# Transposing 20 of 48 groups of softmax numerators on VectorE and GpSimd instead of TensorE, in a four-layer decoder trunk

## The chip, the cores and the metric

The kernel runs on one core of a Trainium2 chip. The metric is the device time of one execution in microseconds. Runs of one kernel agree within about 0.2%. Profiles come from one further execution with the hardware profiler on.

## What is computed

A residual stream of 256 rows by 1024 columns in float32 goes through four layers, each a token mixer and a squared-ReLU MLP. Mixers 0 and 3 are differential attention (8 heads, each the difference of two softmaxes), mixer 1 is block-sparse attention whose block is as long as the sequence, so that only causal attention is left of it (16 heads), and mixer 2 is attention in a window of 128 with sinks (16 heads on 2 key heads).

```python
def reference(x, positions, ...):
    cos, sin = rope_tables(positions)
    h = x
    for i in range(DEPTH):
        a = rms_norm(h, attn_norm_g[i])
        y = (diff_attention, moba_attention, swa_sink_attention)[i % 3](a, ..., cos, sin)
        h = h + y
        h = h + sqrelu_mlp(rms_norm(h, mlp_norm_g[i]), mlp_w_up[i], mlp_w_down[i])
    return rms_norm(h, final_norm_g)

# differential attention, per head and block of queries
    p = jax.nn.softmax(jnp.where(causal, s, -jnp.inf), axis=-1)
    p = p[:, :, 0] - lam * p[:, :, 1]
    o = jnp.einsum('bhqk,bkhe->bqhe', p.astype(v.dtype), v)
    o = rms_norm(o, sub_g) * (1.0 - lambda_init)
```

(The mixers are picked by a tuple here for brevity, and "..." stands for the parameters.)

## The kernel before, in words

All large products are float32 as two parts of a shorter type: for each piece of weights (`raw`, 128 x 1024, brought by one DMA of SyncE's queue) ScalarE writes the high part `whi`, and VectorE subtracts it to get the low part `wlo`. TensorE multiplies three combinations of parts. The two splits, 374 of each, are the steady work of ScalarE and VectorE through the whole kernel. TensorE multiplies from a layer's input projection (`p_in`), through attention, output projection (`p_d`), and MLP (`p_up`, `p_down`), to the next.

Attention lies inside the input projection of its layer: its small steps are put between the projection's matmuls. One step of attention handles one head of a `Diff` layer, or one block of two heads of a `Heads` layer (eight blocks). It goes so:

- `rope` (L589, VectorE: `ropea`, two of `ropeb`, and an addition) turns the first 16 columns of each head's queries and keys, for four heads or blocks at once; `turn` (L694, TensorE) brings queries and keys to columns, in bank `p_qk`; `Queries` (L707) and `put_keys` (L735) split them in high and low parts (`qh`, `qhl`, `kpad`, `kboth`). VectorE makes the low parts; `copied` (L689) puts copies of the high parts beside them, on ScalarE or GpSimd.
- `scores` (L608): TensorE multiplies (`p_s`), VectorE adds the mask and takes the row's least (`ns`, `nm`), ScalarE takes the exponential (`e`) and the sums.
- A `Diff` head combines its two softmaxes on VectorE into one set of numerators, a `Heads` block divides each of its two by its sum (`rl`, on ScalarE or VectorE). One set of numerators is three squares of 128 x 128, since the causal upper square is left out: the tile `e` holds 128 x 384 of them. This is the "group" of the title. There are 8 in layer 0, 16 in layer 1, 16 in layer 2 and 8 in layer 3, 48 in all.
- `turned` (L658): the values are multiplied along the keys, so the group must be transposed. TensorE makes three 128 x 128 transposes into the bank `p_t`, and ScalarE or VectorE copies them out of PSUM to the tile `et`.
- `pair` (L794 for `Diff`, L899 for `Heads`): TensorE multiplies `et` with the values of two heads or blocks into `p_av`. A `Heads` pair is split and stored in `oo` for the output projection; a `Diff` pair is normed by a power that GpSimd takes (`ry`), scaled (`o`), transposed (`p_o`) and stored.

The order is made by a planner, `Plan` (L66). Each piece of work is a task with an engine, a cost, predecessors and a lag after its end; rooms in memory (`et`, `e`, `wk` for PSUM banks, and others) are tokens that a task takes and a later one gives back. `either` and `copied` name tasks with two possible engines. `forth` (L85) builds the order forward in time, choosing for each engine the ready task with the earliest due time, `back` (L148) works out the due times from the end, and the table `EARLIER` shifts the due time of single tasks, by their number. `run` (L177) then issues every task in the order of its planned start. `Ordered` (L198) keeps that order in the program, which is why nearly every instruction bears the line L208. The hardware runs each engine's queue in that order and waits on semaphores alone. The constants `MOVE`, `LATE` and `ASIDE` stand in the file of before without use.

Of the kernel before, what the change touches and what calls it, by code (L numbers as in the profile page):

```python
# [18 lines left out]
P = 128  # L19
# [17 lines left out]
MARGIN = 56  # L37
OWN = 0.08
MOVE = (1.82, 1.95)
LATE = 4.0  # L40
ASIDE = ((0, 2), (0, 1, 2, 3, 4, 5), ())
EARLIER = {4: -7.2, 63: -6, 67: -6.2, 130: -1.4, 132: 3.1, 702: 0.7, 2508: 7.4, 2574: -1.3, 2675: -2.1, 4095: -0.9,
           4105: -5.225, 4107: -23.3, 4167: -3.1, 4176: 4, 4179: -7.9, 4180: 10.7, 4196: -23.9, 4270: 0.9, 4296: -7.5,
           4306: -5.2, 4309: -1.1, 4443: -7.1, 7311: 2.4}


def f(ap):
# [167 lines left out]
def trunk(ctx: ExitStack, tc: tile.TileContext, xT, gains, lams, swa_row, fng, weights, out):  # L215
# [19 lines left out]
    def r3(n):  # L235
        return lambda t: t.rearrange("p (a b) -> p a b", a=n)

    plan = Plan({"wk": range(4), "acc": range(2), "raw": range(RAW), "w": range(SPLIT), "e": (4, 5),
                 "et": (6, 7, 12, 13), "q": (2, 3), "o": range(2), "ns": range(2), "sq": range(2)})
    add, give = plan.add, plan.give  # L240


# [20 lines left out]
    def pe(cost, do, after=(), rank=1, **kw):  # L263
        return add("PE", cost, do, after, rank=rank, **kw)
# [393 lines left out]
    def turned(e, to, after):  # L658

        st = {}  # L660

        def do():
            st["p"] = bank("p_t")
            for j in range(3):
                transpose(st["p"][:, P * j:P * j + P], e()[:, 1 + P * j:1 + P * j + P])

        a = pe(0.36, do, after, take={"wk": 1})
        b = either((0.39, 0.48), lambda: A.activation(to(), st["p"][:, :3 * P], AF.Copy),
                   lambda: V.tensor_copy(to(), st["p"][:, :3 * P]), [a])
        give("wk", [b], a)  # L670
        return a, b

    class Keys:

# [82 lines left out]
    class Diff:  # L757
# [4 lines left out]
        def head(self, h, q, k, after):  # L762
            g, l1 = h // 2, {}

            def begin():
                if g not in self.l0:
                    self.l0[g] = tiny.tile([P, 2, NT], F32, tag="l0", name="l0", bufs=3)
                l1[0] = tiny.tile([P, NT], F32, tag="l", name="l", bufs=6)

            st, exps, first = scores(q, k, True, causal, None, lambda c: l1[0] if c else self.l0[g][:, h % 2], after, begin)  # L770

            def combine():
                c2 = tiny.tile([P, NT], F32, tag="c2", name="c2")
# [17 lines left out]
            self.ready[h], self.turn[h] = b, a  # L791
            return first

        def pair(self, g, v, after):  # L794
            st = {}

            def values():
                p = st["p"] = bank("p_av")
                for h in range(2):
                    et = self.et[2 * g + h]  # L800
                    o = [p[:, S * h + P * t:S * h + P * t + P] for t in range(NT)]
                    matmul(o[0], et[:, 0:P], v(2 * g + h, 0), True, True)
                    matmul(o[1], et[:, P:2 * P], v(2 * g + h, 0), True, False)
                    matmul(o[1], et[:, 2 * P:3 * P], v(2 * g + h, 1), False, True)

            def squares():
                ss = st["ss"] = tiny.tile([P, 2 * NT], F32, tag="ss", name="ss")
                for t in range(2 * NT):
                    junk = sb.tile([P, P], F32, tag="junk", name="junk", bufs=1)
                    A.activation(junk, st["p"][:, P * t:P * t + P], AF.Square, accum_out=ss[:, t:t + 1])  # L810

            def means():
                l0 = self.l0[g][:, :, :].rearrange("p a b -> p (a b)")
                el = tiny.tile([P, 2 * NT], F32, tag="el", name="el")
                V.scalar_tensor_tensor(el, l0, EPS, l0, op0=OP.mult, op1=OP.mult)
                V.scalar_tensor_tensor(st["ss"], st["ss"], 1.0 / P, el, op0=OP.mult, op1=OP.add)

            def power():
                st["y"] = tiny.tile([P, 2 * NT], F32, tag="ry", name="ry")
                G.tensor_tensor(st["y"], st["ss"], minus_half, op=OP.pow)  # L820

            def scaled():
# [35 lines left out]
    class Heads:  # L858
# [4 lines left out]
        def head(self, b, q, k, after):  # L863
            st2 = {}

            def begin():
                st2["l"] = tiny.tile([P, 2, NT], F32, tag="l", name="l", bufs=6)

            st, exps, first = scores(q, k, True, self.mask, self.sinks and self.sinks(b), lambda c: st2["l"][:, c], after, begin)
            ends, a = [], None  # L870
            for c in range(2):

                def inverse(c=c):
                    if c == 0:
                        st2["rl"] = tiny.tile([P, 2, NT], F32, tag="rl2", name="rl2", bufs=4)
# [7 lines left out]
                def to(c=c):  # L883
                    if (b // 2, c) not in self.et:
                        self.et[b // 2, c] = room(self.turn[b // 2, c].got["et"][0], [P, 2, 3 * P], "et")
                    return self.et[b // 2, c][:, b % 2]
# [4 lines left out]
                if b % 2 == 0:  # L891
                    z.take["et"] = 1
                    self.turn[b // 2, c] = z
                ends.append(z)
                self.ready[b, c] = y
            give("e", ends, first)
            return first

        def pair(self, g, v, shared, after):  # L899
            st = {}  # L900

            def values():
                p = st["p"] = bank("p_av")
                o = r3(2)(p)
                for m, cols in ((0, slice(0, S)), (1, slice(P, S))):
                    k = slice(S * m, S * m + S - P * m)
                    for b in (None,) if shared else range(2):
                        for c in range(2):
                            r, et = slice(HD * c, HD * c + HD), self.et[g, c]
# [12 lines left out]
            a = pe(1.5, values, [*(self.ready[2 * g + b, c] for b in range(2) for c in range(2)), *after],  # L922
                   take={"wk": 1})
            for c in range(2):
                give("et", [a], self.turn[g, c])
# [481 lines left out]
```

## Time and profile before

| quantity | value |
|---|---|
| median of 3 runs (lowest, highest) | 1127.94 us (1127.61, 1129.84) |
| the profiled execution, its own time | 1128.46 us |
| its span in the trace | 1126.7 us |
| granted TensorE clock, mean | 0.999 |
| VectorE busy | 826.7 us, 73% |
| ScalarE busy | 671.0 us, 60% |
| GpSimd busy | 54.1 us, 5% |
| splits: `wlo` on VectorE, `whi` on ScalarE | 443.0 us, 373.9 us |

The profile names engines PE (TensorE), DVE (VectorE), ACT (ScalarE), POOL (GpSimd) and SP (SyncE). A row of a timeline gives the start, the length, the engine and line, the operation with the tile it writes, an arrow and what it reads, the shape, and how many instructions stand in the row ("x4"). A bracket behind it gives the idle time of that engine ahead of the row and what ended it. Rows of groups give the count, then the busy time and the mean of one in ns, then the idle time ahead. Matmuls are pipelined and the lengths of their rows are modelled, so distances between starts say more than lengths.

### The profile page before, as it was taken

Reading aid. Unit: us, or ns where it says so; the run is one execution under the profiler, and the core shown is the slowest. Engines: PE = TensorE matmul, PEld = TensorE weight load, DVE = VectorE, ACT = ScalarE, POOL = GpSimd, SP = SyncE. Lnnn points to the kernel's source line nnn. Section 1 sums busy time; section 2 is a strip of 40 time slices with the busy share of each in tenths; the row PEclk is TensorE's granted clock in tenths of the full one; section 3 lists DMA queues with packets and bytes.
Section 4 is the critical chain, followed back from the end, with each engine's and each line's share of the span. In section 5 each row is a group of like instructions: output and inputs, shape, how many; then the busy total and the mean of one; then the engine's idle time right before and its main releaser. Section 6 shows DMA issues by size and latency. Waiting matters only on the chain.

```text
span 1126.7 us, 16639 instructions
## 1 busy us (share of the span) xinstructions
PE 1117.2 (99%) x6462; PEld 978.6 (87%) x6462; DVE 826.7 (73%) x1396; ACT 671.0 (60%) x1163; POOL 54.1 (5%) x89
## 2 busy tenths in 40 slices
PE   9999999999999999999999999999999999999997
PEld 7889888888888898888888898888888899888886
DVE  8986987656697688765569898765669777877453
ACT  6996665444497765554457965553548776555342
POOL 1010000000100000000011100000010110100000
PEclk9999999999999999999999999999999999999999
DMA  8445455555444455455544265555543544556541
GB/s 313 181 153 172 174 201 185 200 192 187 150 154 150 155 181 209 169 215 175 202 173 145 77 229 189 186 193 204 179 171 123 177 161 177 187 187 206 193 144 38
DMA packets 30031, 198.65 MB, mean 176 GB/s; under 512 B 3456, under 2 KB 4864, under 8 KB 6528
## 3 DMA queue, kind: packets, MB, share of 16 engines
q1 hardware_dynamic: 29664, 197.19, 50.0%
q8 instruction: 51, 0.84, 0.3%
q10 hardware_dynamic: 288, 0.39, 0.1%
q14 instruction: 28, 0.23, 0.1%
HBM read 196.52 MB, written 1.05 MB: 175 GB/s over the span
## 4 chain that ended last, share of the span: by engine, by line
PE 98%; DMA 0%; ACT 0%; issue 0%; DVE 0%; POOLq 0%; POOL 0%; SPq 0%; DVEq 0%
PE p_up L208 32%; PE p_down L208 24%; PE p_in L208 20%; PE p_d L208 8%; PE p_last L208 7%; PE p_s L208 2%; PE p_av L208 2%; PE p_t L208 1%; PE p_qk L208 1%; DMA raw<-in_weights 0%; PE p_o L208 0%; PE p_res L208 0%; ACT hg L208 0%; ACT sq L208 0%; POOLq L1403 0%
## 5 line engine op out<-in xcount | busy, mean ns | idle before, releaser
L208 DVE TENSOR_TENSOR wlo<-raw,whi 128x1024 fp32r<-128x1024 f32 (+1 forms) x374 | 443.0, 1218 | 200.8 <-ACT whi L208 195.8
L208 ACT ACTIVATE whi<-raw 128x1024 fp32r<-128x1024 f32 (+1 forms) x374 | 373.9, 1043 | 249.4 <-issue 90.7
L208 PE MATMUL p_up<-hg,whi 128*128 128x512 f32 x1024 | 240.2, 391 | 0.0
L208 PEld LDWEIGHTS p_up<-hg,whi 128*128 128x128 f32 x1024 | 189.5, 188 | 37.9 <-DVE hg L208 0.7
L208 PE MATMUL p_in<-whi,hg 128*128 128x512 f32 (+1 forms) x672 | 188.6, 393 | 1.1 <-DVE hg L208 1.1
L208 PE MATMUL p_down<-uu,whi 128*128 128x512 f32 x768 | 179.1, 390 | 0.0
L208 PEld LDWEIGHTS p_down<-uu,whi 128*128 128x128 f32 x768 | 142.7, 188 | 28.5
L208 PEld LDWEIGHTS p_in<-whi,hg 128*128 128x128 f32 x672 | 122.1, 189 | 23.9 <-DVE hg L208 1.8
L208 PEld LDWEIGHTS p_up<-hg,wlo 128*128 128x128 f32 x1024 | 127.6, 192 | 2.8
L208 PE MATMUL p_up<-hg,wlo 128*128 128x256 f32 x1024 | 128.5, 283 | 0.0
L208 PE MATMUL p_in<-wlo,hg 128*128 128x512 f32 (+1 forms) x336 | 105.4, 392 | 0.0
L208 ACT ACTIVATE uu<-u 128x512 fp32r<-128x512 f32 x64 | 40.2, 628 | 99.2 <-DVE u L208 99.2
L208 PEld LDWEIGHTS p_down<-uu,wlo 128*128 128x128 f32 x768 | 95.3, 192 | 1.9
L208 PE MATMUL p_down<-uu,wlo 128*128 128x256 f32 x768 | 95.9, 283 | 0.0
L208 PE MATMUL p_d<-oo,whi 128*128 128x256 f32 x512 | 95.2, 287 | 0.0
L208 PEld LDWEIGHTS p_d<-oo,whi 128*128 128x128 f32 x512 | 79.6, 192 | 1.1 <-issue 0.9
L208 PE MATMUL p_last<-whi,uu 128*128 128x512 f32 x256 | 79.1, 390 | 0.0
L208 PE MATMUL p_d<-oo,wlo 128*128 128x256 f32 x256 | 72.5, 283 | 0.0
L208 PEld LDWEIGHTS p_in<-wlo,hg 128*128 128x128 f32 x336 | 61.6, 188 | 11.6 <-DVE wlo L208 0.2
L208 ACT ACTIVATE e<-ns,nm 128x128 f32<-128x128 f32 (+3 forms) x128 | 56.9, 447 | 4.5 <-DVE nm L208 3.3
L208 DVE TENSOR_TENSOR uu<-u,uu 128x512 fp32r<-128x512 f32 x64 | 44.1, 689 | 20.4 <-ACT uu L208 19.7
L208 PEld LDWEIGHTS p_last<-whi,uu 128*128 128x128 f32 x256 | 48.1, 188 | 10.0
(158 smaller groups left out, 1030.1 us busy)
## 6 DMA issues: line engine op xcount, KB each, us to landing
raw<-in_weights SPq DMA_DIRECT2D x183, 1024.0 KB, 4.8
raw<-in_weights SPq DMA_DIRECT2D x8, 256.0 KB, 4.9
hT<-in_xT SPq DMA_DIRECT2D x8, 128.0 KB, 4.5
out<-last SPq DMA_DIRECT2D x2, 320.0 KB, 2.4
bias<-in_swa_row SPq DMA_DIRECT2D x1, 512.0 KB, 5.7
grow<-in_fng SPq DMA_DIRECT2D x1, 512.0 KB, 4.9
out<-last ACTq DMA_DIRECT2D x2, 192.0 KB, 2.3
lv<-in_lams SPq DMA_DIRECT2D x1, 256.0 KB, 10.5
```

What stands on the lines that cost most here:

```text
L208: x = getattr(self.engine, name)(*args, **kw)
```

## The change

The constant `ASIDE`, which now is used, names heads 0 to 3 of layers 0 and 3 (`Diff`) and blocks 0 to 5 of layer 1; layer 2 has none. For a head or block in the list, the new class `Aside` takes the place of `turned`: VectorE transposes the group within 32 x 32 squares, straight from `e` into a tile `squares` of which there is one, and GpSimd then moves each square to its place in `et`, four copies for each of four bands of 32 rows, so 16 for a head (32 x 96 elements each) and 16 for a block, after both of its transposes (32 x 192 each). So 4 + 12 + 4 = 20 groups leave TensorE. In the planner the value products are held back by `LATE`, 2.5 us behind the last copy.

The columns of `et` are in an order that suits these copies, and all groups of a layer are read in that order: the value products take strided operands. In layer 2 a pair's value products, formerly one matmul for both blocks, become one for each block. Some small tiles get more buffers, `EARLIER` is another table (two of its numbers are shown), and the space set aside for dynamic DMA is halved. No DMA is added or taken away.

```diff
-LATE = 4.0
-ASIDE = ((0, 2), (0, 1, 2, 3, 4, 5), ())
-EARLIER = {4: -7.2, 63: -6, ...}
+LATE = 2.5
+ASIDE = ((0, 1, 2, 3), (0, 1, 2, 3, 4, 5), ())
+EARLIER = {23: -3.7, 727: -0.5, ...}
...
+    class Aside:
+        def __init__(self, heads, to):
+            self.heads, self.to, self.s, self.squares = heads, to, None, []
+        def turn(self, c, e, after):
+            def do():
+                if self.s is None:
+                    self.s = sb.tile([P, 4, self.heads * 3, 32], F32, tag="turn", name="squares", bufs=1)
+                V.transpose(self.s[:, :, 3 * c:3 * c + 3].rearrange("p k j q -> p j k q"),
+                            e()[:, 1:1 + 3 * P].rearrange("p (j k q) -> p j k q", j=3, k=4))
+            t = dve(384, do, after, 0.08, take=None if self.squares else {"turn": 1})
+            self.squares.append(t)
+            return t
+        def move(self):
+            last = []
+            for a in range(4):
+                def do(a=a):
+                    to = self.to()
+                    for k in range(4):
+                        G.tensor_copy(to[32 * k:32 * k + 32, a], self.s[32 * a:32 * a + 32, k])
+                last.append(add("POOL", MOVE[self.heads - 1], do, [*self.squares, *last[-1:]],
+                                take=None if last else {"et": 1}))
+            give("turn", last, self.squares[0])
+            return last[0], add("POOL", 0.0, lambda: None, last, lag=LATE)
...
-            a, b = turned(lambda: st["e"][:, 0], to, [a])
-            a.take["et"] = 1
+            if h in ASIDE[0]:
+                x = Aside(1, lambda: to().rearrange("p (j a q) -> p a j q", j=3, a=4))
+                a = x.turn(0, lambda: st["e"][:, 0], [a])
+                self.turn[h], self.ready[h] = x.move()
+            else:
...
-                z, y = turned(lambda c=c: st["e"][:, c], to, [z, self.turn.get((b // 2, c))])
+                if aside:
+                    z = aside.turn(c, lambda c=c: st["e"][:, c], [z])
+                else:
+                    z, y = turned(lambda c=c: st["e"][:, c], lambda c=c: to_part(c), [z, self.turn.get(b)])
...
+            if aside:
+                self.turn[b], self.ready[b, 0] = aside.move()
+                self.ready[b, 1] = None
...
-                            if shared:
-                                matmul(o[r, :, cols], v(m, c), et[:, :, k], m == 0, m == 1)
+                            et = self.et[2 * g + b].rearrange("p (a c j q) -> p a c j q", a=4, c=2, j=3)
+                            x = v(m, c if shared else 2 * (2 * g + b) + c)
+                            if m:
+                                matmul(o[r, b, :, 1], x, et[:, :, c, 2], False, True)
                             else:
-                                matmul(o[r, b, cols], v(m, 2 * (2 * g + b) + c), et[:, b, k], m + b == 0, m == 1)
+                                matmul(o[r, b], x, et[:, :, c, 0:2], b == 0, False)
```

Counts of instructions, before and now: on TensorE 144 and 84 transposes into `p_t`, and 16 and 32 value products in layer 2. On VectorE 17 and 7 copies of `et`, no and 20 transposes into `squares`, 14 and 6 scalings of numerators. On ScalarE 31 and 21 copies of `et`, 50 and 58 scalings, 6 and 14 copies of `qhl`, 24 and 20 of `kboth`. On GpSimd 26 and 18 copies of `qhl`, none and 4 of `kboth`, none and 224 of `et`.

The rows below show the order on VectorE in layer 1, shortly ahead of the work for block 4's queries; numbers behind names count the tiles, `raw57` is a piece of weights, `oo` belongs to the pair of blocks ahead, and "waits" lists the counters that an instruction waits for. Before:

```order
L208 TENSOR_TENSOR oo_3470<-p_av_3448,oo_3470 128x2x256 [waits Activation_49]
L208 TENSOR_TENSOR oo_3474<-p_av_3461,oo_3474 128x2x256 [waits Activation_49]
L208 TENSOR_TENSOR wlo57_3495<-raw57_3260,whi57_3494 128x1024 [waits DMAHW1_49,PE_49,Activation_49]
L208 TENSOR_TENSOR wlo57_3495<-raw57_3260,whi57_3494 128x1024 [waits Activation_49]
L208 TENSOR_TENSOR ropea_3539<-qk_3527,cc_126 128x256 [waits Activation_49]
L208 TENSOR_TENSOR ropeb_3540<-qk_3527,nsn_128 128x16x8
L208 TENSOR_TENSOR ropeb_3540<-qk_3527,sn_127 128x16x8
L208 TENSOR_TENSOR qk_3527<-ropea_3539,ropeb_3540 128x16x16 [waits DVE_49]
```

And now:

```order
L207 TENSOR_TENSOR wlo57_3518<-raw57_3302,whi57_3517 128x1024 [waits Activation_49]
L207 STREAM_TRANSPOSE squares_3556<-e_3441 128x3x4x32 [waits DVE_49,Activation_49,Pool_49]
L207 TENSOR_TENSOR oo_3558<-p_av_3538,oo_3558 128x2x256 [waits Activation_49]
L207 TENSOR_TENSOR ropea_3597<-qk_3585,cc_126 128x256 [waits Activation_49]
L207 TENSOR_TENSOR ropeb_3598<-qk_3585,nsn_128 128x16x8
L207 TENSOR_TENSOR ropeb_3598<-qk_3585,sn_127 128x16x8
L207 TENSOR_TENSOR qk_3585<-ropea_3597,ropeb_3598 128x16x16 [waits DVE_49]
L207 STREAM_TRANSPOSE squares_3556<-e_3441 128x3x4x32
```

A block's first transpose, which waits for GpSimd (`Pool`), has moved in ahead of `rope`; the second stands behind it.

The second place is VectorE further on in layer 1, ahead of the scores of block 6, whose queries and keys are `qhl` and `kboth`. Before:

```order
L208 COPY et_3704<-p_t_3673 128x384
L208 TENSOR_TENSOR ropea_3714<-qk_3696,cc_126 128x256 [waits Activation_49]
L208 TENSOR_TENSOR ropeb_3715<-qk_3696,nsn_128 128x16x8
L208 TENSOR_TENSOR ropeb_3715<-qk_3696,sn_127 128x16x8
L208 TENSOR_TENSOR qk_3696<-ropea_3714,ropeb_3715 128x16x16 [waits DVE_49]
L208 TENSOR_TENSOR wlo60_3712<-raw60_3478,whi60_3711 128x1024 [waits DMAHW4_49,PE_49,Activation_49]
L208 SCALAR_TENSOR_TENSOR qhl_3740<-p_qk_3729,qh_3739 64x2x256 [waits Activation_49]
L208 SCALAR_TENSOR_TENSOR qhl_3740<-p_qk_3729,qh_3739 64x2x256
L208 TENSOR_TENSOR kboth_2984<-p_qk_3734,kpad_2983 64x2x256 [waits PE_49,Activation_49]
L208 TENSOR_TENSOR kboth_2984<-p_qk_3734,kpad_2983 64x2x256
```

And now:

```order
L207 RECIPROCAL rl2_3762<-l_3707 128x2 [waits Activation_49]
L207 TENSOR_TENSOR wlo59_3654<-raw59_3463,whi59_3653 128x1024
L207 STREAM_TRANSPOSE squares_3816<-e_3706 128x3x4x32 [waits Activation_49,Pool_49]
L207 SCALAR_TENSOR_TENSOR qhl_3813<-p_qk_3794,qh_3812 64x2x256 [waits Activation_49]
L207 SCALAR_TENSOR_TENSOR qhl_3813<-p_qk_3794,qh_3812 64x2x256
L207 TENSOR_TENSOR kboth_3036<-p_qk_3801,kpad_3035 64x2x256 [waits PE_49,Activation_49]
L207 TENSOR_TENSOR kboth_3036<-p_qk_3801,kpad_3035 64x2x256
L207 STREAM_TRANSPOSE squares_3816<-e_3706 128x3x4x32
```

Here too a transpose that waits for GpSimd stands directly ahead of the queries and keys, where a subtraction of weights stood.

The third place is GpSimd in layer 3, from its first copies of queries to the last power; an ISA row without a tile changes GpSimd's code library. Before:

```order
L208 CAST qhl<-qh 64x2x256 x4
L208 ISA
L208 TENSOR_TENSOR ry<-ss,minus_half 128x4 x2
L208 CAST qhl<-qh 64x2x256 x4
L208 TENSOR_TENSOR ry<-ss,minus_half 128x4 x2
```

And now:

```order
L207 CAST qhl<-qh 64x2x256 x2
L207 COPY et<-squares 32x3x32 x12
L207 CAST kboth<-kpad 64x2x256 x2
L207 COPY et<-squares 32x3x32 x36
L207 ISA
L207 TENSOR_TENSOR ry<-ss,minus_half 128x4
L207 COPY et<-squares 32x3x32 x16
L207 TENSOR_TENSOR ry<-ss,minus_half 128x4
L207 CAST qhl<-qh 64x2x256 x2
L207 TENSOR_TENSOR ry<-ss,minus_half 128x4 x2
```

The change of library stood behind two pairs of casts; it now stands behind the copies of three heads, and the fourth head's copies stand between the first two powers.

More of the change, by code (lines that the diff above doesn't have):

```diff
@@ L238, in trunk @@
     plan = Plan({"wk": range(4), "acc": range(2), "raw": range(RAW), "w": range(SPLIT), "e": (4, 5),
-                 "et": (6, 7, 12, 13), "q": (2, 3), "o": range(2), "ns": range(2), "sq": range(2)})
+                 "et": (6, 7, 12, 13), "q": (2, 3), "o": range(2), "ns": range(2), "sq": range(2), "turn": range(1)})
     add, give = plan.add, plan.give
@@ L665, in do, with put @@
                 transpose(st["p"][:, P * j:P * j + P], e()[:, 1 + P * j:1 + P * j + P])
+        def put(copy):
+            o, x = to(), st["p"][:, :3 * P]
+            copy(o, x.rearrange("p (j m) -> p j m", j=3) if len(o.shape) == 3 else x.rearrange("p (j a q) -> p j a q", j=3, a=4))
         a = pe(0.36, do, after, take={"wk": 1})
-        b = either((0.39, 0.48), lambda: A.activation(to(), st["p"][:, :3 * P], AF.Copy),
-                   lambda: V.tensor_copy(to(), st["p"][:, :3 * P]), [a])
+        b = either((0.39, 0.48), lambda: put(lambda o, x: A.activation(o, x, AF.Copy)), lambda: put(V.tensor_copy), [a])
         give("wk", [b], a)
         return a, b
+    class Aside:
[21 more added lines that the diff above has]
+            return last[0], add("POOL", 0.0, lambda: None, last, lag=LATE)
     class Keys:
@@ L787, in head @@
             a = dve(384, combine, [*exps, made["lam"]], 0.73)
-            a, b = turned(lambda: st["e"][:, 0], to, [a])
-            a.take["et"] = 1
+            if h in ASIDE[0]:
[3 more added lines that the diff above has]
+            else:
+                a, self.ready[h] = turned(lambda: st["e"][:, 0], lambda: to().rearrange("p (j m) -> p j m", j=3), [a])
+                a.take["et"] = 1
+                self.turn[h] = a
             give("e", [a], first)
-            self.ready[h], self.turn[h] = b, a
             return first
@@ L818, in power @@
             def power():
-                st["y"] = tiny.tile([P, 2 * NT], F32, tag="ry", name="ry")
+                st["y"] = tiny.tile([P, 2 * NT], F32, tag="ry", name="ry", bufs=4)
                 G.tensor_tensor(st["y"], st["ss"], minus_half, op=OP.pow)
@@ L866, in begin, with to, to_part @@
             def begin():
-                st2["l"] = tiny.tile([P, 2, NT], F32, tag="l", name="l", bufs=6)
+                st2["l"] = tiny.tile([P, 2, NT], F32, tag="l", name="l", bufs=9)
             st, exps, first = scores(q, k, True, self.mask, self.sinks and self.sinks(b), lambda c: st2["l"][:, c], after, begin)
             ends, a = [], None
+            def to():
+                if b not in self.et:
+                    self.et[b] = room(self.turn[b].got["et"][0], [P, 4 * 2 * 3 * 32], "et")
+                return self.et[b]
+            def to_part(c):
+                return to().rearrange("p (a c j q) -> p c j a q", a=4, c=2, j=3)[:, c]
+            aside = Aside(2, lambda: to().rearrange("p (a j q) -> p a j q", a=4, q=32)) if b in ASIDE[
+                1 + (self.sinks is not None)] else None
             for c in range(2):
@@ L874, in inverse @@
                     if c == 0:
[L875 removed]
+                        st2["rl"] = tiny.tile([P, 2, NT], F32, tag="rl2", name="rl2", bufs=7)
                     V.reciprocal(st2["rl"][:, c], st2["l"][:, c])
@@ L903, in values @@
                 p = st["p"] = bank("p_av")
[L904 to L907, printed above, removed]
+                o = p.rearrange("p (b j a q) -> p b a j q", b=2, j=2, a=4)
+                for m in range(2):
+                    for b in range(2):
                         for c in range(2):
-                            r, et = slice(HD * c, HD * c + HD), self.et[g, c]
-                            if shared:
-                                matmul(o[r, :, cols], v(m, c), et[:, :, k], m == 0, m == 1)
+                            r = slice(HD * c, HD * c + HD)
+                            et = self.et[2 * g + b].rearrange("p (a c j q) -> p a c j q", a=4, c=2, j=3)
+                            x = v(m, c if shared else 2 * (2 * g + b) + c)
+                            if m:
+                                matmul(o[r, b, :, 1], x, et[:, :, c, 2], False, True)
                             else:
-                                matmul(o[r, b, cols], v(m, 2 * (2 * g + b) + c), et[:, b, k], m + b == 0, m == 1)
+                                matmul(o[r, b], x, et[:, :, c, 0:2], b == 0, False)
             def high():
@@ L923, in pair @@
                    take={"wk": 1})
-            for c in range(2):
-                give("et", [a], self.turn[g, c])
+            for b in range(2):
+                give("et", [a], self.turn[2 * g + b])
             hi = act(512, high, [a], PSUM)
```

37 lines of the change are left out of this document (16 added, 21 removed).

## The prediction, made before the result

> **What bounds the kernel now.** I read the busy times on the page first, then the list of TensorE's waits, then TensorE's timeline.
>
> ```profile
> PE 1117.2 (99%) x6462; PEld 978.6 (87%) x6462; DVE 826.7 (73%) x1396; ACT 671.0 (60%) x1163; POOL 54.1 (5%) x89
> PE p_in L208 <- DVE hg L208: 1.1, 1, 1.1
> ```
>
> The first line is part 1 of the page, the second one of the two entries in the list of TensorE's waits (sum, count, largest; the other is of the same size and also at the start). TensorE is the bound from end to end and waits for nobody after its first microseconds. So work taken off TensorE shortens the kernel one for one, as long as nothing new makes TensorE wait; and every such wait is added in full, because TensorE's queue is in order.
>
> **What leaves TensorE.** Its timeline in layer 1 (start, length, matmuls) prices one group of `p_t`, three transposes:
>
> ```profile
> 327.78 1.07 PE L208 MATMUL p_in<-whi,hg 128*128 128x512 f32 x4
> 328.69 0.62 PE L208 MATMUL p_in<-wlo,hg 128*128 128x512 f32 x2
> 329.14 0.84 PE L208 MATMUL p_in<-whi,hg 128*128 128x512 f32 x3
> ...
> 333.56 0.84 PE L208 MATMUL p_in<-whi,hg 128*128 128x512 f32 x3
> 334.24 0.49 PE L208 MATMUL p_t<-ident,e 128*128 128x128 f32 x3
> 334.49 0.48 PE L208 MATMUL p_in<-whi,hg 128*128 128x512 f32 x1
> 334.80 0.63 PE L208 MATMUL p_in<-wlo,hg 128*128 128x512 f32 x2
> 335.27 0.49 PE L208 MATMUL p_t<-ident,e 128*128 128x128 f32 x3
> ```
>
> Lengths are modelled and overlap, so I use starts. Six main matmuls take 329.14 - 327.78 = 1.36 us. With one group among six it is 335.27 - 333.56 = 1.71 us. A group costs 0.35 us, and 20 groups 7.0 us.
>
> The value products of layer 2 become eight matmuls a pair where there were four; those of layer 1 have that shape already:
>
> ```profile
> 338.66 2.82 PE L208 MATMUL p_av<-et,v 128*64 128x256 f32 x32
> 615.50 1.51 PE L208 MATMUL p_av<-et,vkq 128*64 128x512 f32 x8
> ```
>
> Layer 1's two pairs take 2.82 us, 1.41 each; layer 2's pair takes 1.51. I credit 0.1 us for each of four pairs, 0.4 us. The new operands are read and written in strides that the trace does not show; the bounds are a gain of 0.4 and a loss of the same. **Off TensorE: 7.4 us.**
>
> **What is added, and where it stands.** VectorE gets 20 transposes; it and ScalarE lose 20 copies out of PSUM. ScalarE also takes over copies of `qhl` that GpSimd hands back. GpSimd gets 224 copies: 16 for each of 8 heads (32 x 96 elements) and of 6 blocks of two heads (32 x 192). No DMA is moved past anything that waits. None of this is on the path by its length; it matters through two things.
>
> First, *VectorE now waits for GpSimd*. There is one tile `squares`, so a block's first transpose cannot start before the last copy of the block ahead. The rows of the order put that waiting transpose ahead of `rope` in one place and ahead of `qhl` and `kboth` in another, and TensorE's `p_qk` and `p_s` wait for these.
>
> Second, *GpSimd and VectorE exclude each other*:
>
> ```profile
> L208 POOL COPY ns<-rest x16: 184/187/980, 600.9 to 636.8; 128x2 f32<-128x2 f32 x16
> 604.21 1.22 DVE L208 TENSOR_TENSOR wlo<-raw,whi 128x1024 fp32r<-128x1024 f32 x1
> 604.78 0.69 POOL L208 COPY ns<-rest 128x2 f32<-128x2 f32 x1 [3.54 <-ACT e L208]
> 960.52 2.13 POOL L208 PARTITION_ALL_REDUCE rows<-acc  x1 [38.13 <-DVE acc L208]
> 960.97 3.19 DVE L208 TENSOR_TENSOR wlo<-raw,whi 128x1024 fp32r<-128x1024 f32 x2
> ```
>
> A small GpSimd copy takes 0.187 us; one that began under a `wlo` subtraction ended at 605.47, 0.04 us after it. Two `wlo` that began under a reduction took 3.19 us instead of 2 x 1.23. The Trainium skill (SBUF — State Buffer, "SBUF: two separate sides") says that a VectorE instruction with two SBUF inputs and a GpSimd one that reads SBUF take a shared pair of ports in turn, each for its whole length. The trace agrees, and this rule speaks against the change: copies and subtractions queue behind each other.
>
> **Prices.** The new operations are bounded by these rows (GpSimd's two timeline rows, then VectorE's groups, where the number behind the bar's comma is ns of one):
>
> ```profile
> 624.60 1.27 POOL L208 CAST qhl<-qh 64x512 fp32r<-64x512 f32 x2 [8.07 <-ACT qh L208]
> 625.94 0.30 POOL L208 COPY ns<-rest 128x2 f32<-128x2 f32 x2
> L208 DVE TENSOR_TENSOR wlo<-raw,whi 128x1024 fp32r<-128x1024 f32 x366 | 437.5, 1229 | 200.8 <-ACT whi L208 195.8 <-issue 3.0 <-PE p_up L208 0.6
> L208 DVE SCALAR_TENSOR_TENSOR qhl<-p_qk,qh 64x512 fp32r<-64x512 f32 x32 | 22.0, 688 | 5.2 <-ACT qh L208 4.9
> L208 DVE TENSOR_TENSOR kboth<-p_qk,kpad 64x512 fp32r<-64x512 f32 x24 | 16.5, 688 | 1.0 <-ACT kpad L208 0.3
> L208 DVE COPY et<-p_t 128x384 f32<-128x384 f32 x17 | 8.9, 551 | 0.7 <-PE p_t L208 0.6
> L208 DVE TENSOR_TENSOR oo<-p_av,oo 128x512 fp32r<-128x512 f32 x8 | 5.4, 684 | 0.4 <-ACT oo L208 0.4
> L208 DVE RECIPROCAL rl<-l 128x2 f32<-128x2 f32 x32 | 5.2, 162 | 3.8 <-ACT e L208 3.5
> L208 DVE TENSOR_TENSOR ropea<-qk,cc 128x256 f32<-128x256 f32 x12 | 5.1, 425 | 7.2 <-ACT qk L208 7.0
> L208 DVE TENSOR_TENSOR ropeb<-qk,sn 128x128 f32<-128x128 f32 x12 | 3.4, 286 | 0.0
> L208 DVE TENSOR_SCALAR e<-e,rl 128x256 f32<-128x256 f32 x7 | 2.4, 349 | 0.0
> ```
>
> Two casts of 512 elements fill 624.60 to 625.94: 0.67 us each, 1.3 ns an element. By that pace a copy of 192 costs 0.25 us, one of 96 0.125. A line through the 512 and the small copy (0.12 us from start to start) gives 0.325 and 0.22; the slope of recorded lengths alone, (617-187)/510 ns, gives 0.16 for 192. I take the pace, as the cast is the nearest row in kind, and keep 0.16 and 0.325. A transpose I take as the copy of the same shape, 0.55 us; 0.35 to 0.75 are its bounds. `rope` is two instructions of 0.425 and two of 0.286, 1.42 us, all with two SBUF inputs.
>
> **Layer 1, the first wait.** These rows are TensorE's marks (the scores `p_s` of blocks 0, 4 and 6, block 4's second group, the `p_qk` ahead of block 4):
>
> ```profile
> 314.01 0.39 PE L208 MATMUL p_s<-kpad,qh 128*128 128x512 f32 x1
> 353.11 1.05 PE L208 MATMUL p_qk<-ident,qk 128*128 128x128 f32 x8
> 357.44 0.39 PE L208 MATMUL p_s<-kpad,qh 128*128 128x512 f32 x1
> 363.32 0.49 PE L208 MATMUL p_t<-ident,e 128*128 128x128 f32 x3
> 372.32 0.39 PE L208 MATMUL p_s<-kpad,qh 128*128 128x512 f32 x1
> ```
>
> Count from block 0's scores. A block's second group is divided 363.32 - 357.44 = 5.9 us after its scores, so with a transpose and a hand-over the copies start at 6.5. Sixteen copies are 4.0 us; by the order three `wlo` (3.7) and a `rope` (1.4) stand beside them and a pair of casts (1.34) among them; each of four interruptions hides 0.14 us (the small copy needed 0.04 of its 0.187). Block 0 ends at 6.5 + 4.0 + 5.1 + 1.3 - 0.5 = 16.4. Block 1: two transposes and hand-overs 1.3, then 4.0 + 3.7 - 0.4 = 7.3: 25.0. Block 2: its first transpose (0.55) waits for that, then a reciprocal (0.16), two scalings (0.35 and at most the same) and the second transpose (0.55), 2.1 with a hand-over, and 7.3: 34.4. Block 3: transpose 0.55, `oo` 0.68, `rope` 1.42, hand-overs 0.2: `p_qk` can start at 37.2. TensorE reaches it at 353.11 - 314.01 = 39.1, less eight groups (2.8) and one pair of values that now comes later (1.4): 34.9. **TensorE waits 2.3 us.**
>
> **The second wait.** Count from block 4's scores. Copies from 6.5, 4.0 us, with two `wlo` and a `rope` (3.9) beside them, less 0.4: done at 14.0. Then transpose 0.55, two `qhl` and two `kboth` 2.75, hand-overs 0.3: block 6's `p_s` can start at 17.6. TensorE reaches it after 372.32 - 357.44 = 14.9, less four groups, plus the values moved here: still 14.9. **TensorE waits 2.7 us.**
>
> **Layers 0 and 3** turn one group a head, and four heads each:
>
> ```profile
> 43.00:79.00 36.00, 36.00 (x196) 30.15 (x194) 32.34 (x93) 34.00 (x89) 4.12 (x4) 1.00 0.44 154
> 43.00:79.00 36.00, 12.14 (x39) 7.08 (x39) 13.30 (x12) 1.00 0.44 154
> ```
>
> These are a stretch of layer 0, all work and `wlo` alone (VectorE 32.34 and 13.30 of 36 us). Sixty-four copies need 8 us (14 by the line), which fits beside 13.3 us of `wlo`: no wait. What remains is that a copy in flight holds up VectorE's two-input instructions ahead of `p_qk`. A `rope` of four, met by a copy about half the time for half of its 0.125 to 0.25 us, loses 0.1 to 0.3; over some five places I take 0.6 us (0 to 1.5).
>
> **Sum:** -7.4 + 2.3 + 2.7 + 0.6 = -1.8. The profiled execution took 1128.46 us (span 1126.7), which gives 1126.7; it lies 0.5 above the median of the runs, 1127.94, which gives 1126.1. I state the median: **1126.1 us**. Where a stall goes: the small waits of `p_t` for its numerators vanish with it, and what is late next is VectorE behind GpSimd.
>
> **Rivals.**
> 1. *Cheap copies.* At 0.16 us the first wait is nothing and the second 1.3: -7.4 + 1.3 + 0.6 = -5.5, 1122.4 us. For it: the short memory part that the 0.04 us suggests. Against: casts keep 0.67 us from start to start.
> 2. *GpSimd becomes the bound of layer 1* (slower). At 0.325 us the waits are 5.9 and 3.9: +3.0, 1130.9 us. It decides from about 0.28 us a copy, where the two waits eat the gain. For it: the fixed part in the small copy's row. Against: small copies overlap one another (0.12 us between starts, 0.187 long).
> 3. *A change of GpSimd's code library without cover.*
>
> ```profile
> 877.35 1.06 POOL L208 TENSOR_TENSOR ry<-ss,minus_half 128x4 f32<-128x4 f32 x1 [14.19 <-DVE ss L208]
> 873.70 1.50 PE L208 MATMUL p_av<-v,et 128*128 128x128 f32 x12
> 880.40 0.60 PE L208 MATMUL p_o<-ident,o 128*128 128x128 f32 x4
> ```
>
> In layer 3 the order puts an ISA instruction, which readies the power, between block copies and `ry`. Here `ry` came 14.19 us after GpSimd's last work, so the cost of that change lies anywhere from nothing to 14 us, hidden. From a pair's values to its `p_o` 6.7 us were enough. In the changed order 26 main matmuls (5.9), a `p_qk` (1.05) and the values (1.5) make 8.4, so 1.7 us of cover stay and each further microsecond is TensorE's wait. I take no cost in the sum; as a rival I set the load at 6 us, somewhat under half of the bound: 4.3 us of waiting, 1130.4. The Trainium skill (GPSIMD Engine Reference, "Instruction dispatch") gives about 6 us for the first call after such a change, by which 1130.4 would be the forecast; no run here shows it uncovered.
> 4. *Nothing to gain*, because transposes hid in other gaps: the starts above speak against it (0.35 us each).
>
> **Chances.** Forecast (copies 0.22 to 0.28) 0.40, of which 0.18 faster and 0.22 within; cheap copies 0.22; GpSimd as the bound 0.15 (0.12 slower); the library 0.20 (0.02, 0.08, 0.10); nothing to gain 0.03. A measurement of this kernel can tell about 0.2%, 2.3 us, from no change. So faster 0.42, within 0.36, slower 0.22. The range takes in both ends of the copy's price and the library: 1121.8 to 1131.0.
>
> **What would show it.** TensorE's waits: two new ones in layer 1, `p_qk` and `p_s` for VectorE, 2 to 3 us each; `squares` on VectorE ended by GpSimd's `et`; copies of 0.25 us, longer under `wlo`; the span between `p_s` marks otherwise shorter by 0.35 us a group. Wrong if TensorE waits at `p_av` instead, if `p_o` in layer 3 waits for `ry`, or if no wait appears at all.

## The result and the profile after

| | median us | range | ratio to before, 95% interval |
|---|---|---|---|
| before | 1128.17 | 1127.61 to 1129.84 (4 runs) | |
| changed | 1141.92 | 1141.36 to 1142.50 (4 runs) | 1.0119 (1.0102 to 1.0137) |

The change makes the kernel 13.75 us slower, where 1.8 us faster was forecast and 1131.0 was the upper end of the range. The changed kernel's page, parts 1, 2 (TensorE's clock in 40 slices) and 4, and the waits in its list of TensorE's waits that are behind the first 21 us (sum, count, longest):

```profile
PE 1116.7 (98%) x6434; PEld 977.9 (86%) x6434; DVE 830.7 (73%) x1398; ACT 671.0 (59%) x1165; POOL 155.2 (14%) x309
PEclk9999999999999999999999999999999899999999
PE 89%; POOL 4%; DVE 3%; issue 2%; ACT 1%; DMA 0%; SPq 0%; POOLq 0%; DVEq 0%
PE p_o L207 <- DVE o L207: 6.8, 1, 6.8
PE p_qk L207 <- DVE qk L207: 4.7, 2, 4.4
PE p_s L207 <- DVE qhl L207: 0.8, 1, 0.8
PE p_s L207 <- DVE kboth L207: 0.6, 2, 0.4
```

Three things are to be seen. TensorE now waits 12.9 us in layers 1 and 3, where it waited for nothing before. Its busy time fell by 0.5 us only, though 20 groups at 0.35 us left it: something else made its instructions longer. And one slice of its clock is below 9, where all 40 were at 9. In part 4, the chain of work that ended last now has 4% on GpSimd and 3% on VectorE, where both had 0%. These lines of before stand against it:

```profile
PEclk9999999999999999999999999999999999999999
PE 98%; DMA 0%; ACT 0%; issue 0%; DVE 0%; POOLq 0%; POOL 0%; SPq 0%; DVEq 0%
```

The losses lie in two layers: from the first input matmul to the first of the MLP, layer 1 took 116.8 us in place of 110.2 and layer 3 took 116.8 in place of 109.5, while layer 0 took 110.8 in place of 111.5 and layer 2 71.4 in place of 71.1.

Layer 1, GpSimd's and VectorE's timelines of the changed kernel:

```profile
330.91 8.86 POOL L207 COPY et<-squares 32x192 f32<-32x192 f32 x16 [1.14 <-DVE squares L207]
341.63 8.75 POOL L207 COPY et<-squares 32x192 f32<-32x192 f32 x16 [1.86 <-DVE squares L207]
345.42 4.96 POOL L207 COPY et<-squares 32x192 f32<-32x192 f32 x13
350.41 0.58 DVE L207 STREAM_TRANSPOSE squares<-e 128x384 f32<-128x384 f32 x1 [5.24 <-POOL et L207]
350.91 0.65 DVE L207 TENSOR_TENSOR oo<-p_av,oo 128x512 fp32r<-128x512 f32 x1
351.49 0.41 DVE L207 TENSOR_TENSOR ropea<-qk,cc 128x256 f32<-128x256 f32 x1
```

The sixteen copies of block 2 end at 350.38. VectorE has stood still for 5.24 us until then, with the transpose of block 3 at the head of its queue and `rope` behind it: the first wait of the prediction, at the place that it named. The third row is the same block from its fourth copy on, in a window of its own: 13 copies, (4.96 - 0.34)/12 = 0.385 us from start to start (0.34 is the length of one).

Layer 3, GpSimd's timeline, and TensorE at `p_o`:

```profile
882.87 8.02 POOL L207 COPY et<-squares 32x96 f32<-32x96 f32 x16 [0.68 <-DVE squares L207]
897.95 1.05 POOL L207 TENSOR_TENSOR ry<-ss,minus_half 128x4 f32<-128x4 f32 x1 [7.05 <-issue]
898.98 6.69 POOL L207 COPY et<-squares 32x96 f32<-32x96 f32 x16
899.78 1.11 PE L207 MATMUL p_o<-ident,o 128*128 128x128 f32 x4 [6.84 <-DVE o L207]
```

Between the last copy and `ry` GpSimd waited 7.05 us for nothing that the profile shows ("issue"): that is the place of the ISA instruction in the order. The power came late by that, the scaling by it too, and `p_o` waited 6.84 us.

The windows around the two long waits (length, then busy time and instructions of PE, PEld, DVE, ACT, POOL, then the granted clock, DMA share and GB/s), and TensorE's rows behind the first:

```profile
350.00:352.00 2.00, 0.00 (x0) 0.00 (x0) 1.59 (x4) 0.00 (x0) 0.35 (x1) 1.00 0.00 0
354.00:356.00 2.00, 2.00 (x6) 1.62 (x6) 1.96 (x4) 1.95 (x5) 1.80 (x5) 0.50 0.00 0
358.00:360.00 2.00, 2.00 (x13) 1.75 (x12) 0.35 (x1) 1.67 (x2) 1.83 (x5) 1.00 0.43 61
898.00:908.00 10.00, 8.22 (x34) 6.92 (x35) 7.32 (x16) 3.21 (x8) 7.04 (x17) 0.74 0.21 63
353.81 1.63 PE L207 MATMUL p_in<-whi,hg 128*128 128x512 f32 x3
355.24 1.05 PE L207 MATMUL p_in<-wlo,hg 128*128 128x512 f32 x2
356.09 1.53 PE L207 MATMUL p_in<-whi,hg 128*128 128x512 f32 x4
```

During the wait in layer 1 the clock stays at 1.00. Then, with TensorE back at work, it is at 0.50: five main matmuls take 356.09 - 353.81 = 2.28 us, 0.46 each, where the prediction's rows have six in 1.36, 0.23 each. In layer 3 the clock is down before the wait ends (0.59 in the window from 896 to 898) and stays down for some 3.4 us behind it. This is the third loss, and it hides in the busy time.

### The profile page after: what moved, and what is told of

Same layout as the page of the kernel before. It is cut to its first block, busy times and chain, and to the rows that moved or that the text cites. A ratio compares the mean times of both kernels' runs of the same rounds, so it can differ in the third digit from the quotient of the medians.

```text
span 1139.7 us, 16825 instructions
## 1 busy us (share of the span) xinstructions
PE 1116.7 (98%) x6434; PEld 977.9 (86%) x6434; DVE 830.7 (73%) x1398; ACT 671.0 (59%) x1165; POOL 155.2 (14%) x309
## 4 chain that ended last, share of the span: by engine, by line
PE 89%; POOL 4%; DVE 3%; issue 2%; ACT 1%; DMA 0%; SPq 0%; POOLq 0%; DVEq 0%
PE p_up L207 31%; PE p_down L207 23%; PE p_in L207 13%; PE p_d L207 8%; PE p_last L207 7%; POOL et L207 4%; PE p_s L207 2%; PE p_av L207 2%; PE p_qk L207 1%; PE p_t L207 1%; DVE wlo L207 1%; ACT e L207 1%; DVE squares L207 0%; PE p_o L207 0%; DMA raw<-in_weights 0%
## 5 line engine op out<-in xcount | busy, mean ns | idle before, releaser
L207 PEld LDWEIGHTS p_in<-whi,hg 128*128 128x128 f32 x672 | 124.5, 191 | 24.6 <-DVE hg L207 1.1
L207 POOL COPY et<-squares 32x96 f32<-32x96 f32 (+1 forms) x224 | 101.2, 452 | 45.9 <-DVE squares L207 31.4
L207 POOL MEMSET kpad<- 64x512 f32 x8 | 4.2, 520 | 463.9 <-PE p_down L207 463.7
L207 ACT ACTIVATE e<-ns,nm 128x256 f32<-128x256 f32 (+3 forms) x128 | 57.0, 448 | 15.7 <-DVE nm L207 14.4
```

What stands on the lines that cost most here:

```text
L207: x = getattr(self.engine, name)(*args, **kw)
```

## The experiments

### Is it the change of library in layer 3?

A power on one column, behind the first pair of `qhl` casts of layer 3 on GpSimd, makes the library change there, where GpSimd has nothing to do.

```diff
-        t.ways["POOL"] = 0.14 + 0.00234 * n, lambda: do(G.tensor_copy)
+        def on_pool():
+            do(G.tensor_copy)
+            pooled.append(1)
+            if len(pooled) == 9:
+                G.tensor_tensor(tiny.tile([P, 1], F32, tag="early", name="early", bufs=1), ones[:, :1], minus_half[:, :1],
+                                op=OP.pow)
+        t.ways["POOL"] = 0.14 + 0.00234 * n, on_pool
```

> One power on GpSimd is added in layer 3, right behind the first pair of qhl casts, so that the code library changes while GpSimd has 8 us of nothing to do; all else as in the changed kernel (1141.9 us). Library theory: the 7.05 us between GpSimd's last copy and its first ry go, TensorE's wait of 6.8 us at p_o goes, and the granted clock stays at 1.00 behind it (it was 0.64 and 0.68 for 10 us, which costs some 2 us more): 1133 us, 1132 to 1135. Rival, that o is late in layer 3 because VectorE and GpSimd hold each other up over the copies: the wait stays, 1141 to 1142 us. Second rival, that the library change takes its 7 us off the copies of layer 3 instead: wait moves to p_av, 1138 us or more.

Measured: 1132.45 us (1131.58 to 1132.69), ratio to before 1.0036 (1.0022 to 1.0049): 9.5 us less. GpSimd's timeline in layer 3:

```profile
853.51 1.28 POOL L207 CAST qhl<-qh 64x512 fp32r<-64x512 f32 x2 [8.20 <-ACT qh L207]
862.19 0.59 POOL L207 TENSOR_TENSOR early<-ones,minus_half 128x1 f32<-128x1 f32 x1 [7.40 <-issue]
862.87 4.87 POOL L207 COPY et<-squares 32x96 f32<-32x96 f32 x12
890.33 1.15 POOL L207 TENSOR_TENSOR ry<-ss,minus_half 128x4 f32<-128x4 f32 x1
```

The 7.4 us are still paid, but before the copies begin, and `ry` follows the last copy at once. TensorE's wait at `p_o` is gone from its list. The library theory holds; the input projection of layer 3 went from 88.97 to 80.42 us, 8.55 less: 6.84 of waiting and 1.7 more. The clock accounts for that: in the changed kernel its shortfall (2 us at 0.50 are 1 us short) over the windows from 898 to 904 (0.50, 0.50, 0.70) is 2.6 us, of which 1.7 fall behind the end of the wait at 899.78.

### Is it the copies that hold VectorE in layer 1?

In layer 1 four copies of 128 partitions take the place of sixteen of 32. The squares stay in their rows, so this leaves out the move of the squares.

```diff
+                    if self.heads == 2:
+                        G.tensor_copy(to[:, a], self.s[:, a])
+                        return
                     for k in range(4):
```

> In layer 1 each block's sixteen copies of 32 x 192 become four of 128 x 192, which leaves the squares unmoved; layers 0 and 3 as in the changed kernel (1141.9 us). Theory that the copies' own time is what holds VectorE in layer 1: at 0.385 us from start to start 16 copies are 6.2 us and 4 are 1.5, the transposes find the tile free, the waits at p_qk and p_s (6.2 us together) go with the clock lost behind them (some 4.5 us): 1131 us, 1130 to 1133. Rival, that the place of the transposes ahead of rope and of qhl in VectorE's order is the price whatever GpSimd does: under 3 us saved, 1139 us or more.

Measured: 1131.30 us (1130.35 to 1132.89), ratio 1.0027 (1.0017 to 1.0038): 10.6 us less than the changed kernel. No wait at `p_qk` or `p_s` is left in TensorE's list, with the transposes at the same places in VectorE's order. So the copies' time is the price, and not the order alone.

### Or the one tile of squares?

Every second block of layer 1 gets a tile of its own, in memory that the last pair's output takes later. GpSimd's work stays the same.

```diff
-                    self.s = sb.tile([P, 4, self.heads * 3, 32], F32, tag="turn", name="squares", bufs=1)
+                    begun.append(self.heads)
+                    if self.heads == 2 and begun.count(2) % 2 == 0:
+                        self.s = room(17, [P, 4, 6, 32], "squares")
+                    else:
+                        self.s = sb.tile([P, 4, self.heads * 3, 32], F32, tag="turn", name="squares", bufs=1)
```

> Every second block of layer 1 gets a tile of squares of its own (in memory that the last pair's output takes later), nothing else changes against the changed kernel (1141.9 us). Theory that the one tile is what ties VectorE to GpSimd: a block's first transpose waits for the copies of the block before the last, the wait of 4.4 us at p_qk and those of 1.4 us at p_s go with the clock lost behind them: 1131 to 1134 us. Rival, that GpSimd's queue is the bound of layer 1 (sixteen copies in 8 to 9 us): the waits move to p_av, under 4 us saved, 1138 us or more.

Measured: 1131.96 us (1131.67 to 1133.72), ratio 1.0038 (1.0024 to 1.0052): 10.0 us less. TensorE's list has 0.5 us left at `p_qk` and nothing at `p_s` or `p_av`:

```profile
PE p_o L207 <- DVE o L207: 7.4, 1, 7.4
PE p_in L207 <- DVE wlo L207: 0.8, 2, 0.5
PE p_qk L207 <- DVE qk L207: 0.5, 2, 0.3
```

GpSimd's queue is not the bound of layer 1: with slow copies and a second tile the time is nearly that of fast copies and one tile. What hurt was a wait for GpSimd in VectorE's in-order queue, ahead of work that TensorE needs.

### What does the lower clock cost by itself?

The waits stay, but TensorE makes idle transposes ahead of the matmuls that wait.

```diff
             st["p"] = bank("p_qk")
+            turns_done.append(1)
+            for _ in range(36 if len(turns_done) == 13 else 0):
+                transpose(st["p"][:, :P], ones)
...
+            scores_done.append(1)
+            for _ in range(18 if len(scores_done) == 15 else 0):
+                transpose(st["p"][1][:, :P], ones)
...
                 st["q"] = bank("p_o")
+                for _ in range(56 if self.slot and g == 0 else 0):
+                    transpose(st["q"][:, :P], ones)
```

> The changed kernel (1141.9 us) with idle transposes on TensorE just ahead of the three places where it waits: 36 ahead of p_qk and 18 ahead of p_s in layer 1, 56 ahead of p_o in layer 3, 0.117 us each, so that TensorE is busy while it waits. Clock theory: the granted clock stays at 1.00 through and behind the waits, and the time falls by what the lower clock cost, some 4 to 6 us: 1136 to 1138 us, though no wait is any shorter. Rival, that the low clock in the records is only the idle time seen another way: 1141 to 1143 us.

Measured: 1138.14 us (1137.08 to 1139.48), ratio 1.0091 (1.0076 to 1.0106): 3.8 us less than the changed kernel, just short of the 4 to 6 expected. The stretch behind `p_o`, as for the changed kernel above, and the transposes at `p_s`:

```profile
898.00:908.00 10.00, 8.67 (x45) 7.42 (x46) 9.21 (x21) 4.57 (x11) 6.60 (x17) 1.00 0.25 81
374.59 2.16 PE L207 MATMUL p_s<-ident,ones 128*128 128x128 f32 x18 [1.61 <-DVE qhl L207]
376.50 0.48 PE L207 MATMUL p_s<-kpad,qh 128*128 128x512 f32 x1
```

45 matmuls where there were 34, at a clock of 1.00 and not 0.74. The 3.8 us are less than the 5.1 to which the clock's shortfall adds up in the changed kernel once TensorE is back at work (1.7 at each of the three places). At `p_s` the 18 transposes ran behind the wait and not in it: 1.61 us of waiting and then 376.50 - 374.59 = 1.9 us of idle work. At `p_o` 1.5 us of waiting stayed behind the transposes. Neither wait has a drop of the clock behind it, and no window of layers 1 and 3 is below 1.00.

### How long a stall does it take?

In the kernel before, which has no stall there, TensorE's queue gets one in layer 1: a transpose, a ScalarE copy of its result, GpSimd copies on that, and a transpose of the last. Here is the edit with four copies; the others have 8 and 24.

```diff
             st["p"] = bank("p_qk")
+            turns_done.append(1)
+            if len(turns_done) == 13:
+                still = sb.tile([P, 512], F32, tag="relu", name="still")
+                transpose(st["p"][:, :P], ones)
+                A.activation(still[:, P:P + 1], st["p"][:, :1], AF.Copy)
+                for _ in range(4):
+                    G.tensor_copy(still[:, :P], still[:, P:P + 1].to_broadcast([P, P]))
+                transpose(st["p"][:, :P], still[:, :P])
```

> The kernel before (1128.3 us) with one stall put into TensorE's queue in layer 1, at the place of the wait at p_qk: a transpose, a small ScalarE copy of its result, four GpSimd copies of 128 columns on it, and a transpose that reads the last. At some 0.35 us a copy and 0.6 for the hand-overs TensorE stalls 2 us. If a stall costs its own length alone: 1130.3 us. If any stall halves the clock for some 4 us behind it, 2.2 us more: 1132.5. From the changed kernel's trace (1.5 us without a drop, 1.4 us once with one) I expect the first.

> The same with eight GpSimd copies: a stall of some 3.4 us. By its own length: 1131.7 us. With the clock halved behind it: 1134 us, and windows of 2 us at 0.5 in the record. The changed kernel's stall of 4.4 us showed the drop, so I expect the second.

> The same with 24 GpSimd copies: a stall of some 9 us. By its own length: 1137.3 us. If the loss of clock behind a stall is the same whatever its length: 1139.5 us. If it grows with the stall (as if the clock had to be earned back): 1142 us or more.

| run | stall in the trace | median us | over before (1128.41) | beyond the stall |
|---|---|---|---|---|
| stall_4 | 1.98 | 1132.32 (1130.09 to 1133.92) | 3.9 | 1.9 |
| stall_8 | 3.41 | 1135.78 (1134.69 to 1136.53) | 7.4 | 4.0 |
| stall_24 | 9.13 | 1140.00 (1139.39 to 1140.63) | 11.6 | 2.5 |

The windows behind the stall of stall_8:

```profile
356.00:358.00 2.00, 0.00 (x0) 0.00 (x0) 0.00 (x0) 0.00 (x0) 1.63 (x7) 0.82 0.01 4
358.00:360.00 2.00, 1.79 (x9) 1.80 (x10) 0.00 (x0) 0.37 (x1) 0.15 (x1) 0.50 0.00 0
360.00:362.00 2.00, 2.00 (x7) 1.61 (x6) 1.69 (x3) 1.75 (x4) 1.23 (x2) 0.50 0.00 0
362.00:364.00 2.00, 2.00 (x6) 1.54 (x5) 1.94 (x3) 0.92 (x2) 0.00 (x0) 0.50 0.00 0
364.00:366.00 2.00, 2.00 (x11) 1.66 (x10) 0.35 (x1) 1.74 (x2) 0.00 (x0) 0.97 0.40 61
```

In the traces, the stalls of 3.4 and 9.1 us are followed by some 6 and 3.4 us at half clock: the extra does not grow with the stall. For the long one the clock was down from 356 on, 6 us before TensorE came back at 362.5, and that part cost nothing.

But not all of stall_8's 4.0 us is from its stall. Its profiled execution, at 1136.53 the longest of the four, has a second drop at the start of the kernel, behind a wait of 1.80 us for `hg`:

```profile
8.49 0.73 PE L208 MATMUL p_in<-whi,hg 128*128 128x512 f32 x2 [1.80 <-DVE hg L208]
8.00:10.00 2.00, 1.51 (x5) 1.23 (x6) 2.00 (x7) 1.34 (x3) 0.00 (x0) 0.78 0.98 321
10.00:12.00 2.00, 2.00 (x7) 1.51 (x6) 1.97 (x6) 2.00 (x6) 0.00 (x0) 0.50 0.99 346
```

The two runs at a mean clock of 0.996 took 1134.69 and 1135.19, some 3 us beyond the stall. In stall_24 a wait of 1.93 us at the same place has no drop behind it. The kernel before, without any stall, also has 3 of its 12 runs taken beside these near 1129.9 at a clock of 0.997, against 1127.9 to 1128.5 at 0.998 or 0.999 for the rest; a drop at the start may be the reason, but no trace shows one of these runs.

So stall_4 settles less than its median suggests. Its profiled execution had the clock at 1.00 for as long as TensorE worked and took 1131.19, near the 1130.3 that I expected from the stall's own length. Of its nine runs three took 1130.1 to 1131.2 (clock 0.998 or 0.999), four 1132.2 to 1132.5 (0.997) and two 1133.9 (0.995). The four can be what the kernel before shows without a stall; the two lost more than that. That a stall of 2.0 us lowers the clock in some executions is likely, but not shown. The Trainium skill (TensorE: Matmul & The Clock Gate, "What's actually happening") says that the clock halves after an idle window of about 3.4 us, which runs free of the program, and comes back after a busy one. The half clock and its recovery agree with these rows, and a free-running window would explain why waits of 1.80 and 1.93 us at one place went differently. By that rule a shorter wait should cost its own length alone; the 1.80 us at the start of stall_8 doesn't agree, and the measurement decides.

### Both mends together, and the price of the copies in flight

early_and_two has the early power and the second tile. cheap_everywhere has the early power, one tile, and four copies of 128 partitions in all layers, which again leaves out the move of the squares.

> Both mends in one kernel: the early power in layer 3 and the second tile of squares in layer 1. Theory that the two waits and the clock lost behind them are all that the change lost: the savings of 9.5 and 10.0 us add up, 1141.9 - 19.5 = 1122.4 us, 1121.5 to 1124, faster than the kernel before (1128.3) by 0.4 to 0.6%; no wait of TensorE over 1 us behind the first 10 us. Rival, that a third wait was hidden behind these two (GpSimd's queue, at p_av or in layer 0): 1125 us or more, with a new wait in TensorE's list.

> The early power, and in all layers four copies of 128 partitions in place of sixteen of 32, which leaves the squares unmoved (one tile of squares, as in the changed kernel). It gives the time with GpSimd's copies cut to a quarter. If the copies cost nothing more once the two waits are gone, this is the same as early_and_two within 1 us: 1121.5 to 1123.5 us, which is the whole gain of 20 groups, about 5 to 7 us against before. If copies in flight still hold up VectorE's work ahead of TensorE (0.6 us in the prediction, 0 to 1.5), it is 1 us or more below early_and_two.

| run | median us | ratio to before (1128.41), 95% interval |
|---|---|---|
| early_and_two | 1123.17 (1122.63 to 1123.35) | 0.9951 (0.9938 to 0.9963) |
| cheap_everywhere | 1121.37 (1120.62 to 1122.43) | 0.9937 (0.9924 to 0.9951) |

TensorE's list for early_and_two, without the entry at the start:

```profile
PE p_in L207 <- ACT whi L207: 0.8, 2, 0.4
PE p_qk L207 <- ACT whi L207: 0.3, 1, 0.3
PE p_qk L207 <- DVE qk L207: 0.3, 1, 0.3
PE p_sum L207 <- DVE an L207: 0.2, 1, 0.2
```

The two savings add up (1122.4 expected), no third wait was hidden, and the result beats the kernel before by 5.2 us. cheap_everywhere is 1.8 us faster still, by the medians: about what the small copies cost without a long wait (the two kernels also differ in the second tile). The profiled executions are 2.7 us apart, of which 1.6 us lie in the input projection of layer 0 (83.06 and 81.44 us). Where exactly they arise was not tried.

## Why the prediction was wrong

The ledger, in microseconds, from the medians:

| term | forecast | measured | from |
|---|---|---|---|
| 20 groups off TensorE, less the credit for value products | -7.4 | -7.0 | cheap_everywhere against before |
| copies in flight | +0.6 (0 to 1.5) | +1.8 | early_and_two against cheap_everywhere |
| VectorE's wait for GpSimd in layer 1, with the clock behind it | +5.0 | +10.0 | two_squares against changed |
| library in layer 3, with the clock behind it | 0 (rival: +4.3) | +9.5 | lib_early against changed |
| sum | -1.8 | +14.3 | changed against before: +13.75 |

Two steps failed: the library was put at nothing, which is 9.5 of some 15.5 us between forecast and result, and a wait was priced at its length alone, though the clock fell behind it.

- **What leaves TensorE: right in the sum.** 0.35 us a group from the distances between starts gave 7.0 us, and 7.0 was measured with cheap copies. By layers, from the first input matmul to the first of the MLP, cheap_everywhere gained 2.3, 3.9 and 1.4 us in layers 0, 1 and 3, where 0.35 a group makes 1.4, 4.2 and 1.4, and lost 0.3 in layer 2; so that the sums are equal is in part luck. The credit of 0.4 for value products was not there: a pair of layer 2 took as long as before.

```profile
621.47 1.52 PE L207 MATMUL p_av<-et,vkq 128*64 128x256 f32 x16
```

- **The first and second wait of layer 1: the mechanism and the places right, the price of a copy wrong.** I took 0.25 us for 192 elements, by the pace of a cast, with 0.325 as the upper bound. It was 0.385 from start to start, above both. The bound came from a line between a copy of 128 partitions by 2 elements and a cast of 64 by 512, and a copy of 32 rows need not lie on it. By the prediction's count from block 0's scores, block 2's copies were to end at 34.4 us; they ended at 350.38 - 312.89 = 37.5 (312.89 is the start of block 0's scores in the changed kernel). That made the first wait 4.4 us instead of 2.3. The second was shorter, 0.8 and 0.6 us for 2.7. Block 4's copies ended where I had counted, 13.9 us behind its scores (14.0 forecast): they began 0.7 earlier and took 8.05 us in place of 7.5. But block 6's first `p_s` began at 15.9 and not at 17.6, as it waited for `qhl` only; two later matmuls of it then waited for `kboth`. Waits of 6.1 us in all (0.3 of them at an earlier `p_qk`) were forecast as 5.0, so this step alone would have cost 1 us; that it is no more is luck, as one wait was forecast too short and the other too long. The copies in flight also cost more than their bound, 1.8 for at most 1.5; the price of a copy may be the reason.
- **"Every such wait is added in full": too little.** two_squares saves 10.0 us where the waits that it removes are 5.6 (6.1 less the 0.5 that stays). Of the other 4.4 the clock explains 3.4: its shortfall in the changed kernel is 1.7 us from 352 to 358 (0.91, 0.50, 0.74) and 1.7 from 376 to 382 (0.88, 0.50, 0.76), and neither is there in two_squares. The last 1 us is not explained; single runs of a kernel differ by as much. The two longer stalls put into the kernel before show the same without GpSimd's squares in the way. The prediction had no term for it, and the trace of before, at a clock of 1.00 for as long as TensorE worked, could not give its size. The rule of the Trainium skill quoted above stood ready and was not weighed; a wait of 2.7 us would have been below its window, but the 4.3 us of the library's rival above it.
- **The library: a rival at no cost in the sum, and it came true.** Its place (between block copies and `ry`), its victim (`p_o`) and the cover were named; the load was 7.05 us where I set 6, which is also the figure of the Trainium skill (GPSIMD Engine Reference, "Instruction dispatch"); the measurements, 7.05 and 7.40, are above it. By the same count 7.05 less 1.7 of cover would have made a wait of 5.4; 6.84 was measured, so the cover was nearer to 0.2, and the clock took 1.7 more. The cover was short because the third head's sixteen copies ended at 890.89, 6.4 us behind the start of the pair's values (884.46): with no library at all `ry` could not have begun before that, where in the kernel before it began 3.65 behind them. That `p_o` in layer 3 waits for `ry` was one of the prediction's own signs of being wrong. The error was to leave a known instruction, which the order put without doubt on the path, out of the sum because its price was hidden in the trace of before: a bound of 0 to 14 us is no reason for 0.
- **The chances: two rivals were taken one at a time.** GpSimd in layer 1 and the library in layer 3 are in different layers and exclude nothing. Their costs add up, and the upper end of the range held only the larger of the two.

## What to carry to other kernels

In a kernel that one engine bounds from end to end, an in-order queue that the bound engine depends on must not wait for a slower engine ahead of that engine's work: a second buffer was worth 10 us here, with no less work anywhere. Price a wait of TensorE of 3.4 us or more at its length plus some 2 to 3 us lost to half clock behind it, don't count on a shorter one being free of it (one of 1.80 us was not), and add up rivals that live in different stages. Where GpSimd changes its library, issue a small instruction of the new library while it has nothing to do: 9.5 us for one power on a column.

## What the runs showed of the hardware

- In the traces, TensorE's clock fell to 0.50 during or behind every wait of 3.4 us or more (3.4, 4.4, 6.4, 6.8, 7.4 and 9.1 us). It fell behind one of 1.80 us, but not behind others of 1.5, 1.6, 1.93 and 1.98. And it fell behind three waits close together of 0.8, 0.2 and 0.4 us, in the changed kernel as in lib_early:

```profile
374.00:376.00 2.00, 0.93 (x3) 0.37 (x2) 1.92 (x4) 1.08 (x2) 0.00 (x0) 1.00 0.00 0
376.00:378.00 2.00, 1.63 (x9) 1.43 (x9) 1.95 (x3) 0.00 (x0) 0.99 (x1) 0.88 0.00 0
378.00:380.00 2.00, 2.00 (x6) 1.29 (x6) 1.35 (x9) 1.65 (x8) 1.79 (x6) 0.50 0.00 0
```

- GpSimd's copy of 32 partitions has a large fixed part: 0.385 us from start to start for 192 elements, and (2.99 - 0.26)/9 = 0.303 for 96, by the row below of the changed kernel in layer 0 (0.26 is the length of one). A line through these two makes it some 0.22 us fixed and 0.08 for each 96 elements, an estimate from two points. By it sixteen small copies cost by their number more than by what they move.

```profile
45.57 2.99 POOL L207 COPY et<-squares 32x96 f32<-32x96 f32 x10
```

- The change of GpSimd's library took 7.05 us where TensorE felt it and 7.40 us where it was hidden.
